# Gate and up of four feed-forward networks as seven half-block products instead of eight, down in three parts

## The chip, the cores and the metric

One core of a Trainium2 chip runs the whole program. The metric is device time in microseconds (us) of that core, the median over repeated executions. Five engines take part: TensorE (PE in the profile, its weight loads listed apart as PEld), VectorE (DVE), ScalarE (ACT), GpSimd (POOL), and SyncE (SP), which here only issues DMA transfers.

## The reference, cut to what matters

A batch of one sequence of 512 tokens with 1024 features passes two attention layers and then two layers of a second block. Each layer of the second block is: a feed-forward network (`ffn1`), a recurrent and pooling layer (the mix layer), and a second feed-forward network (`ffn2`). So there are four feed-forward networks, all of the same size, each followed by a layer norm:

```
D_MODEL = 1024
D_FF = ((8 * D_MODEL // 3 + 127) // 128) * 128      # 2816

def swiglu(x, w_gate, w_up, w_down):
    return (jax.nn.silu(x @ w_gate) * (x @ w_up)) @ w_down
```

All values are float32. The 2816 hidden features are 22 tiles of 128, the 1024 input features are 8 tiles of 128 (the k tiles), and the 512 tokens are 4 tiles of 128.

## The kernel before, in words

**Number format.** Every weight matrix is loaded as float32 and split into two float32r parts: `H`, a rounded copy made by ScalarE (L189), and `L`, the remainder, made by VectorE (L190). The activations are split the same way (`xH`, `xL`, L220 and L221). One float32 product is then three TensorE matmuls, H by H, L by H and H by L (`mm3`, L123; all matmuls are issued at L121). `weights` (L180) takes a `raw` buffer (two of them, `n_raw`), issues the load on SP, and fills a pair of buffers `wH`, `wL` (five pairs, `n_pair`). A chunk is 128 partitions by 1024 elements, 512 KB.

**One network** is `ffn` (L1077). The hidden features are done in two parts, of 14 and 8 tiles. In each part, `fm_group` (L1064) makes two tiles (256 columns) of gate and then two of up: the stationary operand is a 128 x 128 block of the weights, the moving operand is `xH` or `xL` with all 512 tokens, and the 8 k tiles times 3 matmuls accumulate in one PSUM bank. From those banks ScalarE makes the sigmoid (L1099), VectorE multiplies it with gate (L1100) and then with up (L1102), ScalarE rounds the result to `hH` (L1103) and VectorE makes `hL` (L1104). After gate and up of a part comes down (L1105 to L1132): for each half `c` of the 1024 output columns, four banks (one for each token tile) accumulate over the part's hidden tiles, and L1129 adds them to `x`. In the last part and half, each token tile is finished by itself, followed by its layer norm (`layer_norm`, L1017).

**The seam between two phases.** A layer norm of a token tile is followed by `prep` (L1011), which puts the tile's transposes into a list, `pending`. `flush` (L106) emits the oldest: `transposed` (L211) is 8 transposes on TensorE into two banks of the pool `pst` and the two splits of each bank into `xH` and `xL`. During the last part's second half, two are flushed (at token tiles 2 and 3). At token tile 3 the first weights of the next phase are loaded (`load_early`, L111). `first_groups` (L1045) then begins the next phase by token halves: with the tokens 0 to 255 (matmuls of 256 columns) for all four tiles, flushing the last two transposes in between, and then with the tokens 256 to 511.

**What sets the order.** Each engine works through its own queue strictly in order. The queues are laid out when the program is built, by a planner that places instructions by the order of the program and by when it expects their inputs. Between `order(True)` and `order(False)` (L97) TensorE keeps the order of the program. A tile with one buffer makes its next writer wait for the last reader. PSUM has four pools of two banks: `banks` (three pools, given out in turn by `bank`, L1003) and `pst`.

**The first network** comes after the attention block, whose memory is given back at L963. There `b2_open` (L987) and `lower_bounds` (L968) follow, with a small load, `lba`, whose result VectorE uses.

Of the kernel before, what the change touches and what calls it, by code (L numbers as in the profile page):

```python
# [75 lines left out]
class Net:  # L76
# [20 lines left out]
    def order(self, on):  # L97
        """Between order(True) and order(False) the tensor engine keeps the order of the program."""
# [21 lines left out]
    def mm(self, out, lhsT, rhs, start, stop):  # L120
        return self.nc.tensor.matmul(out, lhsT=lhsT, rhs=rhs, start=start, stop=stop)  # L121
# [58 lines left out]
    def weights(self, srcs, n):  # L180
        """Loads float32 weights and splits them exactly in two float32r parts."""
        nc, wp = self.nc, self.wp
        raw = wp.tile([P, 1024], F32, name="raw", bufs=self.n_raw)
        for lo, a, b, src in srcs:
            nc.sync.dma_start(raw[:, lo:lo + a * b].rearrange("p (a b) -> p a b", a=a) if a > 1
                              else raw[:, lo:lo + b], src)
# [5 lines left out]

    def wkn(self, W, k0, nk, c0, ncol):
        """W: [K, N] in DRAM; the chunk of k tiles k0.. and columns c0.. as [128, nk, ncol] parts."""
# [6 lines left out]
    def rstd(self, ss, scale, eps):  # L201
        """(ss * scale + eps) ** -0.5, elementwise on a small tile."""
# [7 lines left out]

    def transposed(self, t, src, k0=0, nk=KD):  # L211
        """src: [128 tokens, nk*128] -> xH/xL[:, k0.., token tile t]."""
        nc = self.nc
        for b in range(0, nk, 4):
            ps = self.pst.tile([P, 512], F32, name="tr", tag="b").rearrange("p (k t) -> p k t", k=4)
            for k in range(4):
                nc.tensor.transpose(ps[:, k, :], src[:, (b + k) * P:(b + k + 1) * P], self.ident)  # L217
            dH = self.xH[:, k0 + b:k0 + b + 4, t * P:(t + 1) * P]
            dL = self.xL[:, k0 + b:k0 + b + 4, t * P:(t + 1) * P]
            nc.scalar.activation(dH, ps, AF.Copy)  # L220
            nc.vector.tensor_tensor(out=dL, in0=ps, in1=dH.bitcast(F32), op=ALU.subtract)  # L221
# [1136 lines left out]
```

## Time and profile before

| | before |
|---|---|
| Median of 3 runs | 2541.14 us (2539.75 to 2541.31) |
| Profiled execution: span from first to last instruction | 2542.4 us |
| TensorE busy | 2502.9 us, 98% |
| VectorE busy | 1256.5 us, 49% |
| ScalarE busy | 777.1 us, 31% |
| DMA moved | 228.14 MB, mean 90 GB/s |

No other time of the profiled execution is given beside its span; its span is 1.3 us above the median. A busy TensorE in this table is not TensorE at its peak, since matmuls are pipelined and their ends are modelled: the distance between the starts of neighbouring matmuls tells the pace. The networks lie at about 625 to 994, 1211 to 1584, 1584 to 1957, and 2164 to 2535 us of the span; the mix layers lie in between.

### The profile page before, as it was taken

What the parts mean: (1) busy time and instruction counts of PE and PEld (TensorE: products, weight loads), DVE (VectorE), ACT (ScalarE), POOL (GpSimd) and SP (SyncE); (2) the same over time, 40 slices, a digit from 0 to 9 for tenths busy, and PEclk for the clock granted to TensorE, in tenths of its full rate; (3) what the DMA queues carried; (4) which work ended last, traced back from release to release, by engine and by line L of the source; (5) the groups of instructions that cost most, each with busy time, mean ns of one, the idle gap of its engine ahead of it and who ended that gap; (6) DMA issues with size and microseconds to landing.
All of it is one profiled execution on the core that took longest, in us unless ns stands there. A gap on an engine that the chain in (4) does not pass through costs nothing.

```text
span 2542.4 us, 31348 instructions
## 1 busy us (share of the span) xinstructions
PE 2502.9 (98%) x12662; PEld 2071.2 (81%) x12662; DVE 1256.5 (49%) x2355; ACT 777.1 (31%) x1180; POOL 124.1 (5%) x183
## 2 busy tenths in 40 slices
PE   7999999999999999999999999999999999999998
PEld 6878888788888888887888888888888887888887
DVE  4566565675433336576533335433336576533335
ACT  4444443453322222222322222322222222322221
POOL 2000010000000001012000000000001012000000
PEclk9999999999999999999999999999999999999999
DMA  6322242113332333221433332432333221333332
GB/s 185 99 64 75 63 108 49 59 40 96 111 100 91 91 100 107 69 78 55 124 92 100 91 92 83 116 100 92 91 100 109 67 83 50 108 91 100 92 91 75
DMA packets 204991, 228.14 MB, mean 90 GB/s; under 512 B 35072, under 2 KB 160832, under 8 KB 204334
## 3 DMA queue, kind: packets, MB, share of 16 engines
q1 hardware_dynamic: 197840, 207.36, 27.4%
q10 hardware_dynamic: 5150, 10.34, 1.3%
q0 software_dynamic: 1856, 8.44, 1.1%
q8 instruction: 99, 1.62, 0.3%
q14 instruction: 46, 0.38, 0.0%
HBM read 221.87 MB, written 4.24 MB: 89 GB/s over the span
## 4 chain that ended last, share of the span: by engine, by line
PE 93%; DVE 3%; DMA 2%; ACT 1%; issue 1%; POOL 1%; SPq 0%; ACTq 0%; DVEq 0%; POOLq 0%
PE bk L121 69%; PE mm L121 12%; PE pv L121 3%; PE S L121 3%; PE bh L121 3%; PE tr L331 1%; PE tr L217 1%; DMA raw<-in_w_in_dram 1%; DVE wL L190 0%; ACT wH L189 0%; POOL rr L208 0%; DMA lba<-in_lb_param_dram 0%; POOL us L1266 0%; DVE xL L221 0%; ACT kqh L660 0%
## 5 line engine op out<-in xcount | busy, mean ns | idle before, releaser
L190 DVE TENSOR_TENSOR wL<-raw,wH 128x1024 fp32r<-128x1024 f32 (+1 forms) x358 | 438.6, 1225 | 576.1 <-ACT wH L189 571.1
L121 PE MATMUL bk<-xH,wL 128*128 128x512 f32 (+1 forms) x1792 | 664.9, 371 | 0.0
L121 PE MATMUL bk<-xH,wH 128*128 128x512 f32 (+1 forms) x1792 | 664.6, 371 | 0.0
L121 PE MATMUL bk<-xL,wH 128*128 128x512 f32 (+1 forms) x1792 | 663.5, 370 | 0.0
L189 ACT ACTIVATE wH<-raw 128x1024 fp32r<-128x1024 f32 (+1 forms) x358 | 379.0, 1059 | 780.8 <-PE bk L121 672.4
L121 PEld LDWEIGHTS bk<-xL,wH 128*128 128x128 f32 x1792 | 337.4, 188 | 63.8
L121 PEld LDWEIGHTS bk<-xH,wH 128*128 128x128 f32 x1792 | 337.4, 188 | 63.1
L121 PEld LDWEIGHTS bk<-xH,wL 128*128 128x128 f32 x1792 | 337.3, 188 | 63.0
L121 PE MATMUL bk<-wH,hH 128*128 128x512 f32 x704 | 278.9, 396 | 0.0
L121 PE MATMUL bk<-wH,hL 128*128 128x512 f32 x704 | 278.4, 395 | 0.0
L121 PE MATMUL bk<-wL,hH 128*128 128x512 f32 x704 | 278.4, 395 | 0.0
L121 PEld LDWEIGHTS bk<-wH,hL 128*128 128x128 f32 x704 | 132.2, 188 | 32.0
L121 PEld LDWEIGHTS bk<-wL,hH 128*128 128x128 f32 x704 | 132.3, 188 | 31.8
L121 PEld LDWEIGHTS bk<-wH,hH 128*128 128x128 f32 x704 | 132.3, 188 | 31.7
L121 PE MATMUL mm<-wH,xH 128*128 128x512 f32 (+2 forms) x384 | 148.5, 387 | 2.2 <-DVE ckn L412 1.2
L208 POOL TENSOR_TENSOR rr<-rv,nhalf 128x1 f32<-128x1 f32 (+1 forms) x64 | 58.5, 915 | 1799.7 <-DVE rv L206 1795.7
L121 PE MATMUL mm<-wH,xL 128*128 128x512 f32 (+2 forms) x384 | 139.7, 364 | 0.0
L121 PE MATMUL mm<-wL,xH 128*128 128x512 f32 (+2 forms) x384 | 139.6, 364 | 0.0
L1100 DVE TENSOR_TENSOR s<-bk,s 128x512 f32<-128x512 f32 x88 | 60.5, 688 | 153.7 <-ACT s L1099 153.7
L1102 DVE TENSOR_TENSOR h<-bk,s 128x512 f32<-128x512 f32 x88 | 60.8, 691 | 141.5 <-PE bk L121 141.5
L1103 ACT ACTIVATE hH<-h 128x512 fp32r<-128x512 f32 x88 | 54.8, 623 | 206.9 <-DVE h L1102 206.9
L1099 ACT ACTIVATE s<-bk 128x512 f32<-128x512 f32 x88 | 51.8, 589 | 180.9 <-PE bk L121 180.9
(265 smaller groups left out, 2927.9 us busy)
## 6 DMA issues: line engine op xcount, KB each, us to landing
raw<-in_ffn_gate_dram SPq DMA_DIRECT2D x88, 512.0 KB, 3.8
raw<-in_ffn_up_dram SPq DMA_DIRECT2D x88, 512.0 KB, 3.7
raw<-in_ffn_down_dram SPq DMA_DIRECT2D x88, 512.0 KB, 3.5
raw<-in_w_in_dram SPq DMA_DIRECT2D x64, 512.0 KB, 3.7
raw<-in_w_out_dram SPq DMA_DIRECT2D x32, 512.0 KB, 3.5
raw<-in_w_in_dram SPq DMA_DIRECT2D x16, 256.0 KB, 3.5
w<-in_cmp_w_dram SPq DMA_DIRECT2D x8, 512.0 KB, 4.3
tb<-tab POOLq DMA_DIRECT2D x3, 1024.0 KB, 5.2
```

The source lines that it names most:

```text
L121: return self.nc.tensor.matmul(out, lhsT=lhsT, rhs=rhs, start=start, stop=stop)
L189: nc.scalar.activation(H[:, :n], raw[:, :n], AF.Copy)
L190: nc.vector.tensor_tensor(out=L[:, :n], in0=raw[:, :n], in1=H[:, :n].bitcast(F32), op=ALU.subtract)
L208: nc.gpsimd.tensor_tensor(out=r[:, :n], in0=v[:, :n], in1=self.nhalf[:, :n], op=ALU.pow)
L217: nc.tensor.transpose(ps[:, k, :], src[:, (b + k) * P:(b + k + 1) * P], self.ident)
L331: nc.tensor.transpose(pT[:, j * P:(j + 1) * P], keep["p"][:, j * P:(j + 1) * P], self.ident)
L1099: nc.scalar.activation(s, g[j], AF.Sigmoid)
L1100: nc.vector.tensor_tensor(out=s, in0=g[j], in1=s, op=ALU.mult)
L1102: nc.vector.tensor_tensor(out=h, in0=u[j], in1=s, op=ALU.mult)
L1103: nc.scalar.activation(hH[:, 2 * p + j], h, AF.Copy)
```

## The change

Gate (and likewise up) of 2m feature tiles, m = 2 or 1, is taken as a product of 2 x 2 blocks: the weights are halved by features (two halves of m tiles) and by k (two halves of 4 k tiles), the activations by k and by tokens (256 each). The class `Seven` makes the four result blocks from seven products of sums of blocks. Each product is m x 4 x 3 matmuls of 256 columns.

- **Weights.** Each block is loaded as `raw` into one of five buffers `rs` (`raw_block`). Four sums, S1 to S4, are made in place by VectorE (`sum`), and seven parts (A11, A12, A22, S1 to S4) are split into `wH`, `wL` by `split`, which is the second half of the former `weights`.
- **Activations.** `x_sums` makes T1 to T4, sums of activation blocks, once for each network: eight VectorE subtractions on `x` before the transposes. Ten `turned` (4 transposes and the two splits each) take the place of the last two `transposed` (8 transposes each); `prep_s` keeps only the token tiles 0 and 1 in `pending`.
- **Results.** In PSUM bank A the products 1, 6 and 7 accumulate, and after each of them ScalarE copies the bank (`kept`); B holds product 2, C products 5 and 3, D product 4. A VectorE operation (`put`) makes each of the four result blocks from two operands and writes it to SBUF. Sigmoid, products and splits follow as before, on SBUF operands and blocks of m x 256.
- **Order.** The products of one `Seven` run in the order 1, 2, 4, 6, 5, 7, and product 3 runs after product 1 of the next `Seven`, or after the first chunk of down. At the start of a network gate and up are interleaved by hand with the ten `turned`. TensorE keeps the order of the program through the whole network.
- **Parts.** The hidden tiles are done in three parts of 6 (m = 2, 1), 8 (2, 2) and 8 (2, 2) tiles. `hH` and `hL` become 8 tiles long, the pool `ht` and the layer norm rows get one buffer for each name instead of two.

```diff
+    def turned(self, src, dH, dL):
+
+        nc = self.nc
+        ps = self.pst.tile([P, 512], F32, name="tr", tag="b").rearrange("p (k t) -> p k t", k=4)
+        for k in range(4):
+            nc.tensor.transpose(ps[:, k, :], src[:, k * P:(k + 1) * P], self.ident)
+        nc.scalar.activation(dH, ps, AF.Copy)
+        nc.vector.tensor_tensor(out=dL, in0=ps, in1=dH.bitcast(F32), op=ALU.subtract)
...
-        self.ln = self.pool(es, "ln", bufs=2)
+        self.ln = self.pool(es, "ln")
...
+    def ffn_first(self, l, name):
+
+        return [[self.split(self.raw_block(self.wp, "raw", self.n_raw, self.I[f"{name}_{n}_2"][l], 0, j, 2), 1024) for j in range(2)]
+                for n in ("gate", "up")]
...
+    def x_sums(self, hp, xp):
...
+        ts = hp.tile([P, 8, 512], F32, name="ts", tag="hL")
...
+        for t in (2, 3):
+            v = [ts[:, 4 * (t - 2) + i] for i in range(4)]
+            a0, a1, b0, b1 = x[:, t, 0:512], x[:, t, 512:], x[:, t - 2, 0:512], x[:, t - 2, 512:]
+            for out, p, q in ((v[0], a0, b0), (v[2], a1, a0), (v[1], a1, v[0]), (v[3], v[1], b1)):
+                nc.vector.tensor_tensor(out=out, in0=p, in1=q, op=ALU.subtract)
...
+            turns += [lambda a1=a1, d=d: self.turned(a1, self.xH[:, 4:8, d], self.xL[:, 4:8, d]),
+                      lambda v=v, d=d: self.turned(v[0], self.xH[:, 0:4, d], self.xL[:, 0:4, d])]
+            turns += [lambda v=v, c=c, i=i: self.turned(v[i], oH[:, i - 1, :, c], oL[:, i - 1, :, c]) for i in (2, 1, 3)]
...
+            sets = ((p0, p2), (p1, self.pst))
             hp = self.pool(es, "h")
-            tp = self.pool(es, "ht", bufs=2)
+            tp = self.pool(es, "ht")
...
+            def gate(c, put):
...
+                put(v)
+                s = tp.tile([P, c[3], 256], F32, name="s")
+                nc.scalar.activation(s, v, AF.Sigmoid)
+                nc.vector.tensor_tensor(out=v, in0=v, in1=s, op=ALU.mult)
+
+            def up(c, put):
+                h = tp.tile([P, c[3], 256], F32, name="h")
+                put(h)
+                nc.vector.tensor_tensor(out=h, in0=h, in1=G[c[0]][:, c[1], c[2]], op=ALU.mult)
+                fs = slice(c[4] + c[1].start, c[4] + c[1].stop)
+                nc.scalar.activation(hH[:, fs, c[2]], h, AF.Copy)
+                nc.vector.tensor_tensor(out=hL[:, fs, c[2]], in0=h, in1=hH[:, fs, c[2]].bitcast(F32), op=ALU.subtract)
...
-            for half, nf in enumerate((14, 8)):
+            for part, ms in enumerate(((2, 1), (2, 2), (2, 2))):
...
+                        gg.run(1)
+                        turn()
+                        gg.run(2, turn)
+                        turn()
+                        uu.run(1, turn)
+                        turn()
+                        uu.run(2, turn)
+                        turn()
+                        gg.run(5, turn)
+                        turn()
+                        gg.run(6, turn)
+                        for q, k in ((gg, 4), (gg, 7), (uu, 4), (gg, 3), (uu, 6), (uu, 5), (uu, 7)):
+                            q.run(k)
...
+                        for q in (gg, uu):
+                            q.run(1)
+                            if late:
+                                late.run(3)
+                            for k in (2, 4, 6, 5, 7):
+                                q.run(k)
+                            late = q
...
+class Seven:
...
+        self.raw = {f"{i + 1}{j + 1}": net.raw_block(tp, "rs", 5, W, c0 + i * m * P, j, m) for i, j in ((0, 0), (1, 0), (1, 1), (0, 1))}
...
+        self.sum(*{"S3": ("11", "11", "21", ALU.subtract), "S1": ("21", "21", "22", ALU.add),
+                   "S2": ("22", "22", "11", ALU.subtract), "S4": ("12", "12", "22", ALU.subtract)}[name])
...
+        a, x, b, start = {1: ("A11", "B11", "A", True), 2: ("A12", "B21", "B", True), 3: ("S4", "B22", "C", False),
+                          4: ("A22", "T4", "D", True), 5: ("S1", "T1", "C", True), 6: ("S2", "T2", "A", False),
+                          7: ("S3", "T3", "A", False)}[k]
...
+        for p in range(self.m):
+            if p and between:
+                between()
+            o = ps[:, p * 256:(p + 1) * 256]
+            for j in range(4):
+                c = slice(p * P, (p + 1) * P)
+                for i, (w, v) in enumerate(((H, xH), (H, xL), (L, xH))):
+                    self.net.mm(o, w[:, j, c], v[:, j], start and p + j + i == 0, p + 1 == self.m and j + i == 5,
+                                skip_group_check=True)
...
+        if b == "A":
+            s = self.kept[k] = self.tp.tile([P, 512], F32, name="u2" if k == 6 else "u1")
+            self.nc.scalar.activation(s[:, :self.m * 256], ps[:, :self.m * 256], AF.Copy)
+        if k == 2:
+            put(at(0, 0), v(self.kept[1]), B, ALU.add)
+        elif k == 7:
+            put(at(1, 1), v(self.kept[7]), C, ALU.add)
+            put(at(1, 0), v(self.kept[7]), E, ALU.subtract)
+        elif k == 3:
+            put(at(0, 1), v(self.kept[6]), C, ALU.add)
```

## Rows read from the trace of the kernel before

**Rows 1.** The page: busy time (share of the span) x instructions of each engine; clock granted.
```profile
PE 2502.9 (98%) x12662; PEld 2071.2 (81%) x12662; DVE 1256.5 (49%) x2355; ACT 777.1 (31%) x1180; POOL 124.1 (5%) x183
...
PEclk9999999999999999999999999999999999999999
```

**Rows 2.** The chain that ended last, in order of time: start us, us, what.
```profile
640.63 351.88 PE bk L121 x1566
...
1221.51 350.99 PE bk L121 x1566
1573.38 5.59 PE bk L121 x24
...
1590.37 2.83 PE bk L121 x24
1594.27 350.99 PE bk L121 x1566
```

**Rows 3.** The same chain, 1570 to 1600 us, with the transposes at a seam.
```profile
1589.50 0.87 PE tr L217 x8
```

**Rows 4.** Timeline at a network's first matmuls of 256 columns: start us, us, engine.
```profile
1583.88 0.28 PE L121 MATMUL bk<-xH,wH 128*128 128x256 f32 x1
1583.89 0.19 PEld L121 LDWEIGHTS bk<-xL,wH 128*128 128x128 f32 x1
1584.00 0.28 PE L121 MATMUL bk<-xL,wH 128*128 128x256 f32 x1
1584.01 0.19 PEld L121 LDWEIGHTS bk<-xH,wL 128*128 128x128 f32 x1
```

**Rows 5.** Groups by line and shape: xcount | busy us, mean ns | idle before <-releasers.
```profile
L190 DVE TENSOR_TENSOR wL<-raw,wH 128x1024 fp32r<-128x1024 f32 x352 | 432.1, 1228 | 573.5 <-ACT wH L189 568.5 <-PE bh L121 3.1
L1104 DVE TENSOR_TENSOR hL<-h,hH 128x512 fp32r<-128x512 f32 x88 | 60.6, 689 | 30.7 <-ACT hH L1103 30.7
L1129 DVE SCALAR_TENSOR_TENSOR x<-x,bk 128x512 f32<-128x512 f32 x64 | 42.8, 684 | 32.0 <-PE bk L121 31.8
L1213 DVE TENSOR_TENSOR k<-k,tot 128x256 f32<-128x256 f32 x48 | 20.1, 419 | 0.0
L189 ACT ACTIVATE wH<-raw 128x1024 fp32r<-128x1024 f32 x352 | 373.3, 1061 | 776.0 <-PE bk L121 672.4 <-PE mm L121 25.9 <-DMA raw<-in_w_in_dram 25.1
L1103 ACT ACTIVATE hH<-h 128x512 fp32r<-128x512 f32 x88 | 54.8, 623 | 206.9 <-DVE h L1102 206.9
```

**Rows 6.** VectorE's timeline at the seam of two networks, 1574 to 1592 us.
```profile
1574.10 0.68 DVE L221 TENSOR_TENSOR xL<-tr,xH 128x512 fp32r<-128x512 f32 x1
1574.70 1.27 DVE L1030 SCALAR_TENSOR_TENSOR x<-x,rr,lnb 128x1024 f32<-128x1024 f32 x1
...
1577.61 0.69 DVE L1129 SCALAR_TENSOR_TENSOR x<-x,bk 128x512 f32<-128x512 f32 x1 [1.03 <-PE bk L121]
1578.33 0.69 DVE L1022 BATCH_NORM_STATS2 st<-x 128x6 f32<-128x512 f32 x1
...
1584.10 1.22 DVE L190 TENSOR_TENSOR wL<-raw,wH 128x1024 fp32r<-128x1024 f32 x1
1585.23 0.68 DVE L1129 SCALAR_TENSOR_TENSOR x<-x,bk 128x512 f32<-128x512 f32 x1
...
1589.94 1.28 DVE L1030 SCALAR_TENSOR_TENSOR x<-x,rr,lnb 128x1024 f32<-128x1024 f32 x1 [0.43 <-POOL rr L208]
1591.14 1.22 DVE L190 TENSOR_TENSOR wL<-raw,wH 128x1024 fp32r<-128x1024 f32 x1
```

**Rows 7.** Stages: from:to us, PE, PEld, DVE, ACT, POOL busy (x), clock, DMA share, GB/s.
```profile
1221.00:1373.00 152.00, 152.00 (x716) 125.22 (x716) 63.20 (x72) 46.48 (x58) 0.00 (x0) 1.00 0.34 101
1373.00:1455.00 82.00, 82.00 (x354) 65.99 (x353) 22.98 (x23) 15.43 (x15) 0.00 (x0) 1.00 0.31 96
624.00:640.00 16.00, 12.16 (x95) 11.28 (x94) 9.56 (x21) 4.55 (x9) 0.55 (x1) 0.97 0.68 216
```

**Rows 8.** The chain at the start of the first network, 600 to 660 us.
```profile
630.62 6.87 DMA lba<-in_lb_param_dram
...
638.66 1.97 PE tr L217 x8
```

**Rows 9.** Who waited for whom: us in total, times, longest us.
```profile
ACT wH L189 <- PE bk L121: 672.4, 278, 8.8
DVE hL L1104 <- ACT hH L1103: 30.7, 44, 0.7
```

**Rows 10.** DMA issues: KB each, median us to landing.
```profile
raw<-in_ffn_gate_dram SPq DMA_DIRECT2D x88, 512.0 KB, 3.8
```

More of the change, by code (lines that the diff above doesn't have):

```diff
@@ L178, in row, with split @@
         return r
-    def weights(self, srcs, n):
+    def split(self, raw, n):
         nc, wp = self.nc, self.wp
[L183 to L186, printed above, removed]
         H = wp.tile([P, 1024], F32R, name="wH", bufs=self.n_pair)
@@ L191, in weights @@
         return H, L
+    def weights(self, srcs, n):
+        raw = self.wp.tile([P, 1024], F32, name="raw", bufs=self.n_raw)
+        for lo, a, b, src in srcs:
+            self.nc.sync.dma_start(raw[:, lo:lo + a * b].rearrange("p (a b) -> p a b", a=a) if a > 1
+                                   else raw[:, lo:lo + b], src)
+        return self.split(raw, n)
     def wkn(self, W, k0, nk, c0, ncol):
@@ new lines, in ffn @@
+            X, turns = self.x_sums(hp, tp)
+            G = {}
+            def gate(c, put):
+                g = tp.tile([P, 4, 512], F32, name="G") if c[0] not in G else G[c[0]]
+                G[c[0]] = g
+                v = g[:, c[1], c[2]]
+                put(v)
[9 more added lines that the diff above has]
+                nc.vector.tensor_tensor(out=hL[:, fs, c[2]], in0=h, in1=hH[:, fs, c[2]].bitcast(F32), op=ALU.subtract)
@@ new lines, in ffn @@
+            early = self.loaded(lambda: self.ffn_first(l, name))
+            self.order(True)
+            f0 = 0
+            late = None
+            for part, ms in enumerate(((2, 1), (2, 2), (2, 2))):
+                nf = 2 * sum(ms)
+                last = part == 2
+                hH = hp.tile([P, 8, 512], F32R, name="hH")
+                hL = hp.tile([P, 8, 512], F32R, name="hL")
+                f = 0
+                for m in ms:
+                    gg = Seven(self, tp, X, wg, (f0 + f) * P, m, sets[0], early and early[0], lambda c, put, f=f: gate((f0 + f, *c), put))
+                    uu = Seven(self, tp, X, wu, (f0 + f) * P, m, sets[1], early and early[1],
+                               lambda c, put, f=f: up((f0 + f, *c, f), put))
+                    if early:
+                        turn = lambda n=1: [turns.pop(0)() for _ in range(n)]
+                        gg.run(1)
[11 more added lines that the diff above has]
+                            q.run(k)
+                        assert not turns
+                    else:
+                        for q in (gg, uu):
[5 more added lines that the diff above has]
+                            late = q
+                    late = uu
+                    early = None
+                    f += 2 * m
+                for c in range(2):
+                    pools = (p1, p0) if last and c else sets[c]
+                    ps = [pools[t // 2].tile([P, 512], F32, name="bk", tag="b") for t in range(NT)]
+                    if last and c:
+                        HL = [self.wkn(wd, f0 + 2 * k2, 2, c * 512, 512) for k2 in range(nf // 2)]
+                    else:
@@ L1114, in ffn @@
                                              k == 0, k == nf - 1)
-                    else:
-                        HL = [self.wkn(wd, f0 + 2 * k2, 2, c * 512, 512) for k2 in range(nf // 2)]
-                        self.order(True)
+                            if late:
+                                late.run(3)
+                                late = None
                     for t in range(NT):
-                        if half and c:
+                        if last and c:
                             for k in range(nf):
@@ L1322, in first @@
     if not after:
-        net.next = lambda: net.group_weights(net.ffn_groups(0, "ffn1"))
-    net.attn_layer(1, after or net.prep)
+        net.next = lambda: net.ffn_first(0, "ffn1")
+    net.attn_layer(1, after or net.prep_s)
     net.b1_close()
```

110 lines of the change are left out of this document (72 added, 38 removed).

## Prediction

> **What bounds the kernel now.** I read the page first, then the chain that ended last in order of time, then the groups by shape and the timeline at the seams. The page shows TensorE busy for 98% of the span at the full clock level (2.4 GHz), VectorE half idle, ScalarE two thirds idle [rows 1]. The chain shows the networks as unbroken runs of TensorE: 351 us with 1566 matmuls and nothing else in them [rows 2]. TensorE's pace is therefore what the networks cost. A network has 960 matmuls of 512 columns and 192 of 256 in gate and up, and 528 of 512 in down. The unbroken run holds 1446 of the long ones and 120 of the short ones. If a short one costs half, 350.99 / 1506 = 0.2331 us for 512 columns and 0.1165 for 256. The rows beside it agree: 24 long ones take 5.59 us, 24 short ones 2.83 [rows 2], and neighbouring short ones start 0.12 apart at two decimals [rows 4]. So the columns set the pace. A weight load lasts 0.19 us, longer than that distance, but starts 0.01 us after the matmul before it and is hidden [rows 4].
>
> **1. The products.** For m = 2 a `Seven` has 7 x 2 x 12 = 168 matmuls of 256 columns, for m = 1 it has 84. A network has five groups with m = 2 and one with m = 1, for gate and for up: 1848 matmuls. Before: 960 x 0.2331 + 192 x 0.1165 = 246.2 us. After: 1848 x 0.1165 = 215.3. That is **-30.9** for each network.
>
> A page speaks against this. The Trainium skill, "TensorE: Matmul & The Clock Gate", section "Back-to-back issue gap", says that the spacing in a stream is set by weight load and matmul together, with 81 ns for 128 columns and 131 for 512. A straight line between its figures makes a 256-column matmul 0.75 of a long one, an estimate by which the change would cost some 65 us for each network; the trace disagrees, as 0.1165 is half of 0.2331.
>
> **2. The transposes.** Ten `turned` of 4 transposes replace two `transposed` of 8: 24 more. Eight take 0.87 us on the chain [rows 3], so **+2.6** for each network. With all else hidden the change is worth 28.3 in each network, 113 in all: 2428 is the floor.
>
> **3. VectorE in steady state.** A pair of gate and up with m = 2 has 14 splits and 8 sums of 1024 elements, and 20 operations of 512 (8 puts, 4 + 4 products, 4 `hL`). Operations that don't wait for each other start closer than they last: a split is followed after 1.13 us, a 512 after 0.60; one that needs the result just made starts after 0.72 [rows 6]. I take 22 x 1.13 + 20 x 0.66 (the middle, as about half hang on the one before) = 38.1 us. TensorE needs 336 x 0.1165 = 39.1. Before, VectorE was busy for 63 of 152 us in the same stage [rows 7], so the cover goes from ample to 1 us. Before such a stretch of two pairs comes down, 192 x 0.2331 = 44.8 us, in which VectorE has only 8 splits and 8 additions (14.5). There it can run ahead by the five weight buffers less the one in use: 4 splits and 3 sums in place, 7.9 us. So I cost the throughput of parts two and three at 0. If that cover goes, see the third rival. The pair with m = 1 has 22 operations of 512 (0.60) and 20 of 256 (0.419 in full, say 0.38 [rows 5]): 20.8 against 19.6 of TensorE; with the shorter products around its waits **+2** (0 to 4).
>
> **4. ScalarE, SP, POOL, DMA.** ScalarE has for such a pair 14 x 1.06 + 6 copies and 4 sigmoids at about 0.6 + 4 x 0.62 = 23.3 of 39.1 us [rows 5]; today it mostly waits for TensorE to release a pair [rows 9]. SP issues the same loads and 2 MB more for each network (blocks 11 and 12 of the first gate and up come twice), where DMA is a third busy [rows 7]. With five buffers, block 12 of a `Seven` goes where the one before had block 22, after its sum S4. From there 3.8 us of load [rows 10], 1.06 and 1.23 of split are 6.1; between S2's sum and the product that needs it lie five products, 14 us. Cost 0; a lost cover would be seen as TensorE waiting for ScalarE behind a DMA. POOL gets nothing. The third part of down adds 8 additions of 0.68 [rows 5] in stretches where VectorE is busy for 23 of 82 us [rows 7]: 0.
>
> **5. The waits of product 3.** It accumulates onto bank C, which a put must have read; this put needs ScalarE's copy after product 7. Copy 0.6, put 0.69, and half of an operation in front on each engine (0.53 and 0.57) are 2.4 us, against product 1 of the next `Seven`, 2.8. The cover holds on average and breaks in part of the cases: 8 places in a network at 0.4 = **+3** (0 to 10: 1.2 each when a whole operation stands in front of both). Behind the waiting matmul stands all of TensorE's queue. `h` with one buffer makes a put wait for the `hL` before it, which waits 0.70 for ScalarE [rows 9]; other VectorE work fills that if the planner put it there.
>
> **6. The start of a network.** Here VectorE is already full: from TensorE's start at 1583.88 it has the last layer norm and three splits until about 1592.3, 8.4 us later [rows 6]. Now come, before product 5 of gate (which needs S1 and T1): 8 subtractions and 7 `xL` at 0.60 (9.0), sums S3 and S1 and a split (3.4), two puts and two products (2.6). Together 23.4. TensorE has by then four products and seven `turned`: 11.2 + 3.0 = 14.2. The difference is a wait: **+9** (5 if the results come later and gaps are filled; 14 if sum, ScalarE and split follow in single file and the clock halves for a while). In the first network VectorE already holds TensorE up behind the load of `lba`: TensorE is idle for 16 - 12.16 = 3.8 us [rows 7], and eight transposes then take 1.97 instead of 0.87 [rows 8, 3], the slower clock. Some 5 us of waiting are thus there already: +4 (0 to 9).
>
> **The sum.** -30.9 + 2.6 + 9 + 2 + 3 = -14.3 for three networks, -19.3 for the first: -62. The profiled execution's span is 2542.4, 1.3 above the median; the sum is made of differences, so I take it from the median 2541.1: **2479**. All low ends give -23.3 and -28.3: 2443. All high ends (14 + 4 + 10, in the first network 9 + 4 + 10) leave 0.3 and 5.3: 2535.
>
> **Rivals.**
> *Everything is hidden.* VectorE's order at the start is good and product 3 never waits: 2443, at best 2428. For it: VectorE's steady sum stays below TensorE's. Against: the start's 23.4 against 14.2 is arithmetic of rows, not of order. Chance 0.17.
> *The gain is spent in local waits,* the high ends of 5 and 6 in most places: 2515 to 2536, or no difference (2536 to 2546). For it: single buffers (`h`, `s`, `u1`, `u2`, `G`) and engines that can't pass a waiting instruction. Chance 0.15 and 0.04.
> *VectorE becomes the bound of gate and up: slower.* Place: the sums. If operations follow in single file, each takes its full length and each split of a sum waits for ScalarE: 22 x 1.23 + 20 x 0.69 + 8 x 1.06 + 4 x 0.70 [rows 5, 9] = 52 us for a pair, 13 over TensorE; by 5.5 pairs 72, less the two leads 16, plus the start's 9: 65 against 28.3, 2688 in all. It turns the sign when a pair takes over 45.5 us (39.1 + 35.3 / 5.5), 7 us of idling beyond the 38.1 of part 3. Against it: TensorE's lead of up to four finished pairs of weights. Chance 0.10.
> *Weight loads set the pace of short matmuls.* At the 0.19 of rows 4 for each, gate and up take 351 us instead of 260: 2541 + 4 x 94 = 2915. The 120 short matmuls in the unbroken run speak against it. The page named in part 1 has this mechanism. Chance 0.02.
>
> **How the numbers follow.** Forecast (2455 to 2515) 0.52, all hidden 0.17, spent 0.15, no difference 0.04, slower 0.12. About 0.2% (5 us) is what a measurement of this kernel can tell, so faster is 0.52 + 0.17 + 0.15 = 0.84. The range 2438 to 2530 takes in the forecast and nearly all of its two neighbours, 0.8.
>
> **What would show it.** Right: 7392 gate and up matmuls of 256 columns starting 0.1165 apart, VectorE's busy time up by some 560 us (140 for each network: 77 more of the 1.23, 44 results and 22 others at 0.69) to about 1815, TensorE waiting in gaps of several us in the first 15 us of a network for `xL`, the subtractions or the split of S1, and small waits for puts at product 3. Parts two and three should run nearly unbroken. Wrong: gaps spread evenly over all products of parts two and three (VectorE the bound), short matmuls further apart than 0.12, waits of ScalarE for `rs` loads, or no gaps at the start.

## The result, and the profile after

| | before | after |
|---|---|---|
| Median | 2540.44 us (2539.73 to 2541.31, 4 runs) | 2475.11 us (2472.84 to 2476.74, 4 runs) |
| Profiled execution: span | 2542.4 us | 2471.1 us |

The ratio is 0.9746, with a 95% interval of 0.9732 to 0.976: 65.3 us less, where 62 were forecast (2479). The two profiled executions lie 71.3 us apart, 6 more than the medians, because the one before is longer than its median and the one after, with a time of 2472.84, shorter. All accounts below are of the profiled executions.

The page after: busy times, the granted clock in 40 slices, and the shares of the chain of waits. They answer to [rows 1]; before, the chain was 93% PE and 3% DVE.

```profile
PE 2401.1 (97%) x15542; PEld 2134.4 (86%) x15542; DVE 1766.1 (71%) x3011; ACT 1007.3 (41%) x1524; POOL 125.2 (5%) x183
PEclk9999999999999999999999999999999999999999
PE 84%; DVE 9%; DMA 2%; ACT 2%; issue 2%; POOL 1%; DVEq 0%; SPq 0%; ACTq 0%; POOLq 0%
```

VectorE is busy for 510 us more and now holds 9% of the chain. Where it does so is told by the chain in order of time, here in the second network, which begins at 1189.34 (start, length, what; "xN" counts instructions):

```profile
1196.95 1.28 DVE x L1042
1198.23 0.61 DVE xL L222
1198.84 0.04 issue
1198.88 0.66 PE tr L220 x4
1199.54 2.08 PE bk L121 x12
1201.62 0.85 PE tr L220 x4
...
1204.37 0.44 PE tr L220 x4
...
1209.79 0.68 DVE h L1146
1210.47 3.41 DVE rs L1428 x3
1213.88 0.60 DVE oL L222
1214.48 1.13 DVE wL L186
1215.61 0.61 DVE oL L222
...
1219.16 21.58 PE bk L121 x179
...
1251.68 97.91 PE bk L121 x694
...
1356.88 114.47 PE bk L121 x792
...
1479.71 54.58 PE bk L121 x318
```

Up to 1219 the chain runs through VectorE: layer norm, `xL` and `oL`, sums, splits. Behind that TensorE is nearly alone again: 97.9, 114.5 and 54.6 us in one piece, as the 351 us of [rows 2] were before. Between these pieces the chain runs 7 and 8 us through VectorE, up to the put that a product 3 needs, but TensorE itself waits only 0.3 us there. The windows say the same by stage (columns as in [rows 7]; the last is the start of the fourth network):

```profile
1198.00:1218.00 20.00, 15.96 (x112) 15.12 (x113) 18.74 (x25) 7.60 (x12) 0.00 (x0) 0.89 0.27 89
1217.00:1220.50 3.50, 3.50 (x19) 3.50 (x19) 1.64 (x4) 1.30 (x2) 0.00 (x0) 0.51 0.89 270
1252.00:1350.00 98.00, 98.00 (x699) 91.06 (x698) 78.99 (x100) 46.51 (x62) 0.00 (x0) 1.00 0.38 119
1358.00:1535.00 177.00, 176.90 (x1184) 160.94 (x1182) 129.62 (x150) 71.27 (x86) 1.52 (x2) 1.00 0.36 111
2110.00:2145.00 35.00, 28.16 (x231) 26.71 (x231) 33.89 (x45) 15.58 (x23) 1.45 (x1) 1.00 0.39 123
```

In the start VectorE is busy for 18.74 of 20 us, TensorE for 15.96, at a granted clock of 0.89. In the later parts TensorE is busy throughout, VectorE for 79 of 98 and 130 of 177 us. TensorE's own waits over 0.3 us in this network are these, with the longest of the fourth network as the last line (timeline; behind each the idle time and what ended it):

```profile
1198.88 0.66 PE L220 MATMUL tr<-ident,ts 128*128 128x128 f32 x4 [3.01 <-DVE xL L222]
1209.20 0.38 PE L121 MATMUL bk<-xH,wH 128*128 128x256 f32 x1 [0.69 <-ACT xH L221]
1209.92 0.39 PE L121 MATMUL bk<-xL,wH 128*128 128x256 f32 x1 [0.34 <-DVE xL L222]
1214.76 0.35 PE L121 MATMUL bk<-oH,wH 128*128 128x256 f32 x1 [0.97 <-ACT oH L221]
1216.26 0.38 PE L121 MATMUL bk<-oL,wH 128*128 128x256 f32 x1 [1.15 <-DVE oL L222]
1242.78 0.38 PE L121 MATMUL bk<-xH,wH 128*128 128x256 f32 x1 [0.56 <-DVE h L1472]
1251.68 0.39 PE L121 MATMUL bk<-oH,wH 128*128 128x256 f32 x1 [0.37 <-ACT u L1477]
2120.13 0.66 PE L220 MATMUL tr<-ident,ts 128*128 128x128 f32 x4 [3.09 <-DVE xL L222]
```

The first is the largest. The third group of transposes needs a bank of `pst` back; its reader, the `xL` of the first group, stands in VectorE's queue behind the layer norm of the last token tile and the first subtractions. Behind that wait the clock falls: four transposes take 0.85 us at 1201.62 and 0.44 at 1204.37, half the speed, which is the 1.2 GHz level. Then product 5 waits for T1, and product 6 for T2, whose `oL` stands behind three sums. Behind that wait the clock falls a second time (0.51 from 1217 to 1220.5). Such a wait doesn't always bring the lower level: in the fourth network the same wait is 3.09 us long, and the granted clock stays at 1.00.

**The account.** From the first matmul of a network to the first of the next phase (for the fourth, to the end of the span):

| network | before | after | difference | forecast |
|---|---|---|---|---|
| 1 | 378.4 | 359.3 | -19.1 | -19.3 |
| 2 | 372.7 | 356.3 | -16.4 | -14.3 |
| 3 | 372.8 | 356.3 | -16.4 | -14.3 |
| 4 | 378.8 | 360.6 | -18.2 | -14.3 |

Together -70 of the span's -71.3. What stands outside the networks changed by about 1 us in sum.

### The profile page after: what moved, and what is told of

Read it like the earlier page. It is cut to its first block, busy times and chain, and to the rows that moved or that the text cites. A ratio compares the mean times of both kernels' runs of the same rounds, so it can differ in the third digit from the quotient of the medians.

```text
span 2471.1 us, 38370 instructions
## 1 busy us (share of the span) xinstructions
PE 2401.1 (97%) x15542; PEld 2134.4 (86%) x15542; DVE 1766.1 (71%) x3011; ACT 1007.3 (41%) x1524; POOL 125.2 (5%) x183
## 4 chain that ended last, share of the span: by engine, by line
PE 84%; DVE 9%; DMA 2%; ACT 2%; issue 2%; POOL 1%; DVEq 0%; SPq 0%; ACTq 0%; POOLq 0%
PE bk L121 60%; PE mm L121 12%; PE pv L121 3%; PE S L121 3%; PE bh L121 3%; DVE wL L186 2%; DVE rs L1428 2%; PE tr L338 1%; PE tr L220 1%; ACT wH L185 1%; DVE xL L222 1%; DMA raw<-in_w_in_dram 0%; DMA rs<-in_ffn_up_dram 0%; DMA raw<-in_ffn_up_dram 0%; POOL rr L212 0%
## 5 line engine op out<-in xcount | busy, mean ns | idle before, releaser
L121 PE MATMUL bk<-xH,wH 128*128 128x256 f32 (+1 forms) x1664 | 484.7, 291 | 6.2 <-ACT xH L221 2.7
L121 PE MATMUL bk<-xL,wH 128*128 128x256 f32 (+1 forms) x1664 | 478.3, 287 | 3.2 <-DVE xL L222 3.2
L121 PE MATMUL bk<-xH,wL 128*128 128x256 f32 (+1 forms) x1664 | 478.9, 288 | 0.0
L185 ACT ACTIVATE wH<-rs 128x1024 fp32r<-128x1024 f32 (+1 forms) x320 | 314.1, 984 | 346.8 <-PE bk L121 278.6
L186 DVE TENSOR_TENSOR wL<-rs,wH 128x1024 fp32r<-128x1024 f32 (+1 forms) x320 | 360.0, 1129 | 110.0 <-ACT wH L185 109.9
L121 PE MATMUL bk<-oH,wH 128*128 128x256 f32 x1056 | 297.4, 282 | 5.0 <-ACT oH L221 3.7
L121 PE MATMUL bk<-oL,wH 128*128 128x256 f32 x1056 | 296.8, 281 | 4.4 <-DVE oL L222 4.4
L121 PE MATMUL bk<-oH,wL 128*128 128x256 f32 x1056 | 296.3, 281 | 0.0
L1428 DVE TENSOR_TENSOR rs<-rs 128x1024 f32<-128x1024 f32 (+1 forms) x192 | 217.1, 1134 | 13.4 <-DMA rs<-in_ffn_gate_dram 10.5
L121 PEld LDWEIGHTS bk<-oL,wH 128*128 128x128 f32 x1056 | 199.6, 189 | 5.5 <-DVE oL L222 5.2
```

Source lines behind the costliest of these rows:

```text
L185: nc.scalar.activation(H[:, :n], raw[:, :n], AF.Copy)
L186: nc.vector.tensor_tensor(out=L[:, :n], in0=raw[:, :n], in1=H[:, :n].bitcast(F32), op=ALU.subtract)
L1428: self.nc.vector.tensor_tensor(out=raw[to][:, :n], in0=raw[a][:, :n], in1=raw[b][:, :n], op=op)
```

## The experiments

All but two are edits of the changed kernel; those two are edits of the kernel before. "Before" beside a time is the kernel before on the same chip. Differences to the changed kernel compare medians from different chips, on which the kernel before differs by up to 1.8 us.

**Short matmuls alone.** Is a matmul of 256 columns really half of one of 512, with its weight load hidden? The kernel before, with all of gate and up by token halves:

```diff
-                        g = self.fm_group(wg, (f0 + 2 * p) * P, 256, False)
-                        u = self.fm_group(wu, (f0 + 2 * p) * P, 256, False)
+                        g = self.fm_group(wg, (f0 + 2 * p) * P, 256, True)
+                        u = self.fm_group(wu, (f0 + 2 * p) * P, 256, True)
```

> The kernel before, with all gate and up products by token halves: 960 matmuls of 512 columns in each network become 1920 of 256, with the same columns in all. Theory (columns set the pace, a short matmul costs 0.1165 us, half a long one): no change, 2540 us within 5. Rival (the weight load sets the pace of short matmuls, 0.19 us each): 1920 x 0.19 = 365 instead of 224 us for each network, 564 more in all, about 3105.

2519.28 us (2514.91 to 2523.29), before 2542.21; ratio 0.9912 (0.9894 to 0.9929). Its chain in the first and in the second network:

```profile
638.35 351.22 PE bk L121 x2526
...
1219.07 344.62 PE bk L121 x2526
```

And its groups by shape, where the first of the three kinds of short matmul has no idle time in front:

```profile
L121 PE MATMUL bk<-xH,wH 128*128 128x256 f32 x2944 | 816.6, 277 | 0.0
```

The rival, weight loads that set the pace, is gone: with twice the loads the kernel is 23 us faster, and none of these matmuls waits. Twelve short ones in a row start 1.36 us apart, 0.1133 for one, where half a long one is 0.1167. So 960 long matmuls become 1920 short ones of 0.1133, and a network can lose 960 x (0.2333 - 0.2267) = 6.3 us; the run of 351 us is 344.62. In this execution three networks do. The first does not: the same 2526 instructions take 351.22 us. There the short matmuls of the first part start 0.1178 apart, though they read the same `xH` and `xL`, and those of the second part 0.1133; about 1 us is a stretch at half clock. So the pace is not fixed by the operand, and what picks it is open; that may be why the runs spread from 2514.91 to 2523.29, but only one was profiled. Some 23 us, a third as much as the change brings, was to be had without it; the seven products bring the other 44.

**Three parts alone.** The kernel before with parts of 6, 8 and 8 tiles:

```diff
-            for half, nf in enumerate((14, 8)):
+            for half, nf in enumerate((6, 8, 8)):
...
```

> The kernel before, with the hidden tiles in three parts of 6, 8 and 8 instead of 14 and 8: the third part of down alone, 8 more additions in each network. Theory (VectorE is idle enough there): no change, 2540 us within 5. Rival (each seam of parts makes TensorE wait): 8 additions of 0.69 us in the open are 5.5 for each network, 22 in all, 2562.

2540.79 us; ratio 0.9997 (0.9988 to 1.0006). The third part of down is free, as forecast.

**One product more.** If TensorE's columns are the bound outside the start, an eighth product costs its full time; if VectorE is, it hides. Product 2 is done twice, the second time over the first, in all but the first pair of a network:

```diff
-                            for k in (2, 4, 6, 5, 7):
+                            for k in (8, 2, 4, 6, 5, 7):
...
-                          7: ("S3", "T3", "A", False)}[k]
+                          7: ("S3", "T3", "A", False), 8: ("A12", "B21", "B", True)}[k]
```

> The changed kernel, with product 2 of each Seven done twice, except in the first pair of a network: eight products instead of seven, while VectorE and ScalarE have the same work. It adds 8 x 24 + 2 x 12 = 216 short matmuls to each network. Theory (TensorE's columns are the bound behind the start): 216 x 0.1165 = 25 us for each network, 101 in all: 2576. Rival (VectorE is the bound of gate and up): TensorE has room, most of the added matmuls are hidden and the time rises by less than 50: under 2525.

2572.98 us (2571.46 to 2574.36); ratio 1.0123 (1.0108 to 1.0138), 97.9 us over the changed kernel. That is 4 networks x 216 matmuls x 0.1133 = 97.9. With more time for VectorE in each `Seven`, the chain has no break at all behind the first two pairs:

```profile
1271.87 288.18 PE bk L121 x2108
```

**Product 3 in its own place.** What is it worth that product 3 runs behind product 1 of the next `Seven`?

```diff
-                            if late:
-                                late.run(3)
-                            for k in (2, 4, 6, 5, 7):
+                            for k in (2, 4, 6, 5, 7, 3):
...
```

> The changed kernel, with product 3 right behind product 7 of the same Seven instead of after product 1 of the next. It takes away what covers ScalarE's copy, the put and their queues. Theory (that chain takes some 2.4 us and lies in the open now): 11 places in each network by 2 to 2.4 us, 22 to 26, in all 90 to 105: 2565 to 2580. Rival (the chain is short or hidden in other ways, and the order of product 3 is worth nothing): no change, 2475 within 8.

2647.48 us (2642.3 to 2648.13); ratio 1.041 (1.0393 to 1.0427): 172 us over the changed kernel, slower than the kernel before, and far over either expectation. The group of the matmuls in question, by shape:

```profile
L121 PE MATMUL bk<-xH,wH 128*128 128x256 f32 x1536 | 462.4, 301 | 116.6 <-DVE h L1470 65.8 <-DVE G L1470 47.9 <-ACT xH L221 2.8
```

Three windows around one of the waits:

```profile
1355.00:1364.00 9.00, 6.42 (x56) 6.22 (x54) 8.20 (x9) 4.26 (x5) 0.00 (x0) 0.97 0.10 34
1364.00:1368.00 4.00, 3.91 (x18) 3.92 (x19) 2.36 (x4) 1.26 (x2) 0.00 (x0) 0.50 0.23 54
1368.00:1382.00 14.00, 14.00 (x114) 14.00 (x113) 10.05 (x12) 7.05 (x9) 0.00 (x0) 0.92 0.46 136
```

The puts cost 113.7 us of idle time, some 2.6 for each of 44 places. The chain of copy and put behind product 7 has about the length that part 5 of the prediction gave it, 2.4. What the expectation lacked is the clock: behind this wait it stood at half for four us and at 0.92 over the next 14. Over the whole span the mean granted clock is 0.97, against 0.995; 0.03 of 2646 us less 0.005 of 2471 are some 67 us, which with the 114 make up the 172 and a little more. Moving one product past another hides both.

**The sums left out.** Is it VectorE's amount of work in the start, or something in line? The sums S1 to S4 are not made, so four parts of weights are plain blocks; the rest runs as it is.

```diff
-        self.nc.vector.tensor_tensor(out=raw[to][:, :n], in0=raw[a][:, :n], in1=raw[b][:, :n], op=op)
+        pass
```

> The changed kernel without the four sums S1 to S4 of the weights (their blocks are used as loaded), 48 VectorE operations less in each network, 54 us of VectorE time. Theory (VectorE holds TensorE up only in the first 30 us of a network): only the three sums in the chain there count, 2.5 to 3.4 us for each network and perhaps a little of the pair with m = 1: 10 to 16 in all, 2459 to 2465. Rival (VectorE is the bound of gate and up throughout): most of the waiting that is left, some 12 us for each network, goes: over 35 in all, under 2440.

2476.42 us (2475.28 to 2478.19); ratio 0.9746 (0.973 to 0.9763): no change, against both expectations. 192 operations are gone without effect, and VectorE is busy for 1574.7 us instead of 1766.1. So VectorE's throughput doesn't bound the kernel, and what stood behind the sums was held by other things too. The zero hides a small trade: in the second network product 3 now waits about 0.38 us at each of the six last places, against nothing to 0.28 in the changed kernel; why is not shown. In the timeline the first wait is as in the changed kernel:

```profile
1200.99 1.11 PE L220 MATMUL tr<-ident,ts 128*128 128x128 f32 x4 [3.32 <-DVE xL L222]
```

And where three sums stood in the chain, a load stands now:

```profile
1214.89 4.11 DMA rs<-in_ffn_up_dram
```

**The subtractions left out.** T1 to T4 are transposes of plain blocks, and nothing is subtracted before them:

```diff
-        ts = hp.tile([P, 8, 512], F32, name="ts", tag="hL")
...
-            v = [ts[:, 4 * (t - 2) + i] for i in range(4)]
-            for out, p, q in ((v[0], a0, b0), (v[2], a1, a0), (v[1], a1, v[0]), (v[3], v[1], b1)):
-                nc.vector.tensor_tensor(out=out, in0=p, in1=q, op=ALU.subtract)
+            v = [a0, a1, a0, a1]
```

> The changed kernel without the eight subtractions on x at the start of a network (the tiles of x are transposed as they are), 8 x 0.6 us of VectorE less. Theory (the start is VectorE's queue): the third transposition comes 1.8 us earlier (three subtractions stand in front of its buffer's release), the slow clock behind it shrinks with the wait, and the later ones save up to 2.4: 3 to 6 for each network, 12 to 24 in all, 2451 to 2463. Rival (the start is bound by the last layer norm, the subtractions fill VectorE's gaps): under 4 in all.

2465.51 us (2464.57 to 2466.64); ratio 0.9702 (0.9687 to 0.9716): 9.6 us less, 2.4 for each network on average, below the 12 to 24 expected and above the rival's 4. In the profiled executions the second to fourth networks are 2.4, 4.1 and 1.9 us shorter, the first is 1.4 longer. In the second network the wait at the third transposes falls from 3.01 to 0.81 us, and product 5 then waits longer for its `xL`, 1.60 instead of 0.34:

```profile
1198.14 0.66 PE L220 MATMUL tr<-ident,x 128*128 128x128 f32 x4 [0.81 <-DVE xL L222]
...
1208.76 0.38 PE L121 MATMUL bk<-xL,wH 128*128 128x256 f32 x1 [1.60 <-DVE xL L222]
```

The half clock goes only in part: behind product 5's wait, short matmuls start 0.21 apart for three us, one such stretch instead of two (the third network has none, the first more than before). In the second network most of the 2.2 us taken out of the first wait, and of VectorE's 8 x 0.60, is used up by the next wait.

**The subtractions on GpSimd.** The same eight operations, moved to the idle engine:

```diff
-                nc.vector.tensor_tensor(out=out, in0=p, in1=q, op=ALU.subtract)
+                nc.gpsimd.tensor_tensor(out=out, in0=p, in1=q, op=ALU.subtract)
```

> The changed kernel with the eight subtractions on GpSimd, which takes 1.1 to 1.3 us for such an operation elsewhere in this kernel. Theory (VectorE's queue): GpSimd is free there, the four of the last token tile are done 5 us after its layer norm, before their transposes are due: nearly the gain of leaving them out, 8 to 20 in all, 2455 to 2467. Rival (GpSimd is too slow for the chain of four, or hinders VectorE): no gain, 2475 or more.

2480.8 us (2479.41 to 2482.72); ratio 0.9762 (0.9748 to 0.9777): 5.7 us more than the changed kernel. The rows of the moved operations (shortest, median, longest in ns):

```profile
L1096 POOL TENSOR_TENSOR ts<-x x16: 1262/1294/2302, 627.9 to 2128.5; 128x512 f32<-128x512 f32 x16
```

The chain beside them:

```profile
1196.59 2.26 DVE wL L186
1198.97 2.12 DVE wL L186
...
1207.86 1.69 DVE G L1141
```

GpSimd needs twice as long as VectorE's 0.68, and while it works, VectorE's own operations stretch: a split of 1.23 us takes 2.26. The Trainium skill, "GPSIMD Engine Reference", section "1. Specifications", says that GpSimd shares its SBUF interfaces with VectorE and contends with those of its instructions that read two inputs from SBUF; the split is such a one, and the trace agrees. It also shows the other side: operations that read one operand from PSUM keep their 0.67 to 0.68 us beside GpSimd (the put at 1204.66, the split into `oL` at 1205.26).

**Two other orders of the start.** If waits at the start are a matter of order, TensorE could first do the four products that need no sum of `x`, with each `turned` just ahead of the product that reads it (first edit); or the third to seventh `turned` could come half a product later, when the banks are free (second edit):

```diff
...
                         gg.run(1)
+                        gg.run(2)
+                        uu.run(1)
+                        uu.run(2, lambda: turn(1))
+                        turn(6)
+                        for q, k, mid, end in ((gg, 5, 3, 8), (gg, 6, 4, 9), (gg, 4, 2, 7), (gg, 7, 0, 5)):
+                            q.run(k, lambda: turn(mid))
+                            turn(end)
...
```

```diff
                         gg.run(1)
-                        turn()
                         gg.run(2, turn)
                         turn()
                         uu.run(1, turn)
-                        turn()
+                        turn(2)
```

> The changed kernel with another order at the start: products 1 and 2 of gate and of up first, with no transposes in between but those of T1, then 5, 6, 4, 7 of gate with the transposes of T2, T4, T3 and B22 each in front of the product that needs them. Same work on all engines. Theory (TensorE stands still at the third transposition, which the fourth of the layer norm's successors holds up, and then runs at the slow clock for some 3 us): TensorE has 11 us of products before it needs anything of the late tiles; product 5 comes some 3 to 5 us earlier, 12 to 20 in all, 2455 to 2463. Rival (the sum of VectorE's work before product 5 decides, whatever the order): no change, 2475 within 6.

> The changed kernel with the third to seventh transposition group one half product later at the start of a network: product 1 of up begins before the third, and two stand behind product 2 of up. Theory (up to product 6 VectorE's queue is full and sets the end of the start, whatever TensorE does in between): the first wait shrinks by 1.4 us, the slow clock behind it may go, but product 6 begins at nearly the same time: 0 to 2 us for each network, 2467 to 2475. Rival (each wait of TensorE counts by itself): 1.4 and the 3 us of slow clock for each network, 18 in all, 2457.

The first: 2503.43 us (2502.32 to 2503.61), ratio 0.985 (0.9835 to 0.9864), 28 us worse than the changed kernel, where 12 to 20 better was expected. The wait for the third transposes is gone, but each of the products 5, 6, 4 and 7 now waits for its own operands:

```profile
1213.12 0.39 PE L121 MATMUL bk<-xH,wH 128*128 128x256 f32 x1 [0.69 <-ACT xH L221]
1215.15 0.38 PE L121 MATMUL bk<-xL,wH 128*128 128x256 f32 x1 [1.65 <-DVE xL L222]
...
1223.30 0.36 PE L121 MATMUL bk<-oH,wH 128*128 128x256 f32 x1 [1.13 <-ACT oH L221]
...
1229.69 0.38 PE L121 MATMUL bk<-oH,wH 128*128 128x256 f32 x1 [1.42 <-ACT oH L221]
...
1237.31 0.38 PE L121 MATMUL bk<-oH,wH 128*128 128x256 f32 x1 [1.22 <-ACT oH L221]
```

The second: 2477.79 us (2472.66 to 2481.88), ratio 0.9749 (0.9736 to 0.9762), no difference from the changed kernel. The first wait falls from 3.01 to 1.95 us, and a split of a sum of weights or of a T then ends later waits (1.40 before product 6's first matmul, 0.75 before its third). VectorE's queue sets when the start ends, not the place of single transposes.

**Why are some short matmuls faster than others?** In the changed kernel most of those that read `xH` and `xL` start 0.1133 us apart, those that read `oH` and `oL` (T2 to T4) 0.1167. Three edits: T2 and T3 as halves of rows of 512 elements, as T1 is; down's matmuls as two of 256 columns, 0.1133 each if it is the length; and that with all tiles of the network moved by 32 bytes.

```diff
-        oH = xp.tile([P, 3, 4, 256], F32R, name="oH")
-        oL = xp.tile([P, 3, 4, 256], F32R, name="oL")
+        o = [[xp.tile([P, 4, n], F32R, name=f"o{z}{n}") for n in (512, 256)] for z in "HL"]
+        oH, oL = ([w[:, :, 0:256], w[:, :, 256:512], q] for w, q in o)
...
```

> The changed kernel with another layout of the sums of activations: T2 and T3 side by side as halves of rows of 512 elements, like xH, and T4 alone in rows of 256 as before. In the changed kernel the products that stream xH or xL space their matmuls 0.1133 us, those that stream T2, T3 or T4 0.1167. Theory (the step between the rows of the streamed tile makes the difference): products 6 and 7 go to 0.1133 and product 4 stays at 0.1167; 2/7 of 1848 matmuls by 0.0034 are 1.8 us for each network, 7 in all, 2468. Rival (the place of the tile in memory, or something else that the tiles differ in): no change of the spacing, 2475 within 3.

```diff
+    def mm6(self, out, aH, aL, bH, bL, start, stop):
+        for i, (a, b) in enumerate(((aH, bH), (aH, bL), (aL, bH))):
+            for h in (slice(0, 256), slice(256, 512)):
+                self.mm(out[:, h], a, b[:, h], start and i + h.start == 0, stop and i == 2 and h.start > 0,
+                        skip_group_check=True)
...
```

> The changed kernel with each matmul of down as two of 256 columns, both halves accumulating in the one bank: 1056 short ones instead of 528 long ones in each network, same columns, twice the weight loads. Theory (a short matmul that streams half of a row of 512 costs 0.1133 us, under half of 0.2333): 528 x (0.2333 - 0.2267) = 3.5 us for each network, 14 in all, 2461. Rival (the gain seen with gate and up belongs to xH and not to the length): no change, or slower if the doubled loads show: 2475 or more.

```diff
+        hp.tile([P, 8], F32, name="pad")
         ts = hp.tile([P, 8, 512], F32, name="ts", tag="hL")
```

> The changed kernel with down's matmuls as two of 256 columns, and with every tile of the network's pools moved up by 32 bytes in each partition. In the program's layout xH, xL and all pairs wH, wL begin 32 bytes past a multiple of 64, and oH, oL, hH, hL at a multiple; the short matmuls that start 0.1133 apart are those in which moving and stationary operand stand alike in this (xH on wH), those at 0.1167 (oH on wH) and 0.118 (wH on hH, down in halves) are those in which they differ. With the 32 bytes all stand alike. Theory (the two operands' places in a line of 64 bytes set the spacing): short matmuls on oH, oL come to 0.1133, 3168 x 0.0034 = 11 us in all, and down's pairs to 0.2267 instead of 0.2333, 2112 x 0.0066 = 14 us: 2450 (2444 to 2458), the fastest kernel here. Rival (the region of memory, or the names' other properties, set it): the spacings stay 0.1167 and 0.118, and the time is that of down in halves, 2486. If it holds for gate and up alone: 2475.

Rows of 512: 2479.17 us (2474.22 to 2481.86), ratio 0.9755 (0.9741 to 0.9768), and the distances stay as they were. Down in halves: 2486.18 us (2484.64 to 2487.52), ratio 0.9783 (0.9769 to 0.9796), 11 us slower than the changed kernel where 14 faster was expected; two halves take 0.2366 against 0.2333, which for 2112 pairs is 7 of the 11. Moved by 32 bytes: 2482.81 us (2481.05 to 2484.57), ratio 0.977 (0.9757 to 0.9783), against 2450 expected. The timeline of that last kernel shows that place matters in some way, but not by the rule that was tried ("x2" is the two halves):

```profile
1270.26 0.39 PE L121 MATMUL bk<-wH,hH 128*128 128x256 f32 x2
1270.48 0.39 PE L121 MATMUL bk<-wL,hH 128*128 128x256 f32 x2
...
1289.76 0.40 PE L121 MATMUL bk<-wH,hL 128*128 128x256 f32 x2
1289.99 0.40 PE L121 MATMUL bk<-wH,hH 128*128 128x256 f32 x2
```

In the first chunk of down (at 1270) a pair of halves follows after 0.227 us on average, in nearly all later ones (at 1290) after 0.235, though nothing in the rule tells the chunks apart. Those on `oH` and `oL` went from 0.1167 to 0.1177, the wrong way.

Read by dozens of neighbouring matmuls at the full clock (the first distances of each, which vary, left out), the timelines say more. In the changed kernel itself `xH` and `xL` have two paces: 351 dozens start about 0.1133 apart, 30 start 0.1177 apart (product 3 at 1229.47, say). After the move by 32 bytes all other short matmuls take these same two paces, 0.1133 or 0.1177, and no longer 0.1167 or 0.1183: the halves of down the lower one in 60 dozens and the higher in 292, those on `oH` and `oL` nearly always the higher. So place seems to decide which paces there are (the moved kernel ran on another chip than the one that it is compared with). Which of the two a stretch takes changes where other work comes in between (product 3, transposes), with operands and places as they were; what picks it stays open. Of all runs, only the one that leaves the subtractions out is faster than the changed kernel.

## Why the prediction held

The total was 62 against 65.3, and the parts of the second network come out as follows. The waits are read from the distance between the starts of matmuls, less their pace. That the total came so close is in part luck: the terms miss by up to 2.7 us in both directions.

| term | forecast | found | from |
|---|---|---|---|
| products | -30.9 | -33.6 | 1056 x 0.1133 + 792 x 0.1167 = 212.1, against 960 x 0.2333 + 192 x 0.1133 = 245.7 |
| transposes | +2.6 | +2.6 | 24 more at 0.109 |
| start of the network | +9 | +11.0 | waits 7.4, breaks at the transposes 0.5, two stretches at half clock 3.1 |
| pair with m = 1 | +2 | +1.2 | 0.71 + 0.53 |
| waits of product 3 | +3 | +0.5 | 0.28 + 0.26 at two places |
| not named | 0 | +1.9 | remainder |
| sum | -14.3 | -16.4 | |

**1, the products: right in kind, off by 2.7.** The term assumed that a short matmul is half a long one, 0.1165, which the run of 351 us and the two decimals of [rows 2, 4] could not tell from 0.1133. Four of the seven products read `xH` and `xL` and run at the lower figure nearly always. The rival on weight loads, and with it the straight line between the figures of the Trainium skill, "TensorE: Matmul & The Clock Gate", section "Back-to-back issue gap", fell by the first experiment: there two short matmuls take 0.2267 us, or 0.2356 at their slower pace, where one long one takes 0.2333.

**3, VectorE in steady state: right.** It rests on a sum of 38.1 us against TensorE's 39.1, so little cover that the third rival had a tenth. The unbroken runs of 97.9 and 114.5 us and the full price of an eighth product say that VectorE keeps up; the kernel without the sums says that 191 us less of its busy time change nothing. Its busy time rose by 510 us, not 560: the forecast took each new operation at its full duration, while neighbours overlap, as part 3 itself used (77 x 0.10 + 66 x 0.09 = 13.6 for each network, 55 in all). The groups for it, which answer to [rows 5], show the durations as they were forecast:

```profile
L186 DVE TENSOR_TENSOR wL<-rs,wH 128x1024 fp32r<-128x1024 f32 x264 | 322.2, 1223 | 101.0 <-ACT wH L185 100.9
L1428 DVE TENSOR_TENSOR rs<-rs 128x1024 f32<-128x1024 f32 x160 | 195.1, 1224 | 13.1 <-DMA rs<-in_ffn_gate_dram 10.5
```

**4, ScalarE, SP, DMA and the third part of down: right but for one place.** Down in three parts changed nothing by itself. In the pair with m = 1 ScalarE stands behind a load into `rs`, in each network:

```profile
1247.34 2.78 DMA rs<-in_ffn_up_dram
```

By the chain, the copy that product 7 needs comes late for it: this is the 0.53 us of the table. TensorE waiting for ScalarE behind a load is what the forecast named as the sign of a lost cover; it had put the cost at 0. In the later parts no load stands on the chain.

**5, the waits of product 3: too high, 3 against 0.5.** The price of copy and put was right, as its own experiment showed (2.6 for each place when it lies open), and so was the doubt about the margin; product 1 of the next `Seven` covers it nearly always, not in part of the cases. The 0.71 us in the row above is also a wait of product 3, behind a product 1 of half the length; with it the term would be 1.3.

**6, the start: near in size, the place half right.** The forecast took 23.4 us of VectorE against 14.2 of TensorE before product 5 and made one wait of it. It came as a chain of waits, the largest already before the third transposes, where a PSUM bank comes back late, and 3.1 us of it as a lower clock, which the forecast had only in its high end. That the sums are in the way, which the forecast counted in (3.4 of the 23.4), did not show: without them the start is as long. The subtractions are: 2.4 us for each network on average.

**The first network** gained 19.1, as forecast, because it had some waits already [rows 7, 8]. The fourth gained 18.2, 1.8 more than the second and third. Its start is spared the two stretches at half clock, worth 3.1; somewhat longer waits take part of that back.

What spoke for "everything is hidden" (2443) held in the steady part and failed at the start; "spent in local waits" is what happens, and far beyond its 2536, when product 3 is put in its own place.

## What to carry to other kernels

Where a bound engine's work falls by an eighth and another engine pays with much more, cost the second engine by the distance between starts, not by durations, and stage by stage: here it kept up everywhere but in the first 30 us of each phase. A result that goes through two other engines before the bound one may use its bank again is best given a whole product of other work in between; that one placement was worth 172 us here, more than the change itself. And try a piece of a change alone: shorter matmuls, which need no new algorithm, brought 23 us by themselves, a third as much as the change.

## What the runs showed of the hardware that was not expected

- Two matmuls of 256 columns that read `xH` or `xL` mostly take 0.2267 us, one of 512 takes 0.2333. The same operands also run at 0.1177 each, in one execution through the whole first part of a network. On other moving operands a short one takes 0.1167 or 0.1183, and 0.1133 or 0.1177 after a move by 32 bytes. The row length is not the cause; what picks one of the two paces is open.
- Weight loads of 0.188 us stay hidden under matmuls that start 0.1133 apart, in a run of 2526 of which 2040 are short.
- Beside GpSimd's subtractions a VectorE split went from 1.23 to as much as 2.26 us, and GpSimd's own operations from 1.29 to 2.30.
- After most waits of 2.6 to 3 us the granted clock was at its lower level (1.2 of 2.4 GHz) for three to seven us, but not after the one of 3.09 us in the fourth network; where such waits come 44 times, that added more than half as much again as the waits themselves (some 67 us beside 114).
